# Dilated attention taken two units at a time, and retention outputs transposed in pairs

## The chip, the cores and the metric

The kernel runs on one core of a Trainium2 chip. The metric is device time of one execution in microseconds. Engines are named as in the profile: PE is the matrix engine (TensorE), with PEld for its weight loads; DVE is the vector engine, ACT the scalar engine, POOL GpSimd, and SP the engine whose queue issues most loads.

## What is computed

One layer of a decoder trunk for 512 tokens of 1024 features. The input projection feeds a retention mixer and a dilated attention; both outputs are gated, projected and added, and an MLP and a gated embedding follow. The change touches the dilated attention and the last step of the retention. Their part of the reference, cut:

```python
DIL_GROUPS = ((128, 1), (512, 4), (2048, 16))   # window, dilation; 8 heads of 64 each
def dilated_group(q, k, v, window, dilation):   # keys t - j*dilation, j = 0..window//dilation
    ...
    s = jnp.einsum('bcnqhe,bcnkhe->bcnhqk', qs, kk) * (hd ** -0.5)
    s = jnp.where(mask[None, :, None], s, -1e30)
    pr = jnp.exp(s - lse[..., None])
    o = jnp.einsum('bcnhqk,bcnkhe->bcnqhe', pr, vv)
...
yr = retention(rq, rk, rv, positions)
yr = rmsnorm(yr) * jax.nn.silu(rg)
ya_branch = yr.reshape(B, S, RET_V_W) @ w_ret_out[i]
```

## The kernel before

**Products in three passes.** Each 128x512 block of a large product is three matmuls (`PASSES`, L215): weights and features are split into a high and a low part of type fp32r, the high part by an ACT copy (L66) and the low part by a DVE subtraction (L69). Weights come in blocks of 512 KB through SP's queue (L82) into tiles of the pool `t` (26 tiles, which the attention's tiles share), and `prep_next` splits the next block while PE works.

**Fillers between the products.** `acc_tile` (L234) calls `pump()` after every three matmuls. `pump` hands out queued steps of other work at a given rate. The attention of a head group is such a list of steps: it is spread over 84 calls, and its matmuls stand between those of the next projections. A scheduler then sets the order on each engine from the order of the calls, its own estimate of when operands are there, and priorities; so a step's matmuls may stand some way from where they were handed out, and may be split up.

**One unit of attention.** `unit(t, p0)` covers 128 queries and, for the first head group, four heads (up to 256 keys, two blocks), for the other two groups all eight heads (128 keys). It has three steps. `scores` (matmuls at L475) multiplies q and k in fp32. A head has 64 features, so an instruction uses 64 of the array's 128 rows: even heads the upper half, odd heads the lower half, and each half writes a PSUM bank of its own. Then DVE adds the mask and takes the maximum of each head (L479), and ACT takes the exponentials (through L66). `flip` transposes the weights on PE (L495), and ACT copies them out of PSUM. `weigh` multiplies them with v (L506), and when all eight heads of 128 queries are done, DVE copies the sum (L511).

**Order of steps.** The list takes, for each unit in turn, `weigh` of the unit two before, `flip` of the one before, and `scores` of this one. There are eight units in the first head group and four in each of the other two.

**PSUM.** There are eight banks: four for the large products (`abank`, pool `pacc`), and four for everything else (`bank`, pool `pps`), handed out in turn. A bank is written again only when its reader is done.

**Retention.** At the end of each of four heads, the gated output of 128x512 values for each of four blocks of tokens is transposed by `flip(e)` (L814), four 128x128 transposes for each `e`; ACT copies the bank and sends it to DRAM. The four calls are handed out at 12, 14, 16 and 18 calls of `pump`.

Of the kernel before, what the change touches and what calls it, by code (L numbers as in the profile page):

```python
# [16 lines left out]
S, D, P = 512, 1024, 128  # L17
NT = S // P
# [13 lines left out]
def hybrid_block(ctx, tc, a, out):  # L32
    nc = tc.nc
# [12 lines left out]
    def nm(s):  # L46
        count[0] += 1
        return f"{s}{count[0]}"

    def big(shape=(P, D), dtype=F32):  # L50
        return pt.tile(list(shape), dtype, name=nm("t"), tag="t")

    def half(shape=(P, 512), dtype=F32):
        return psm.tile(list(shape), dtype, name=nm("s"), tag="s")

    def stat(n=1):
        return pst.tile([P, n], F32, name=nm("st"), tag=f"st{n}")

    def bank():
        return pps.tile([P, 512], F32, name=nm("b"), tag="ps")  # L60
# [4 lines left out]
    def act(o, i, f=AF.Copy, **kw):  # L65
        nc.scalar.activation(o, i, f, **kw)  # L66
# [39 lines left out]
    def new_w():  # L106
        return pw.tile([P, 2, 2, 512], F32R, name=nm("w"), tag="w")
# [90 lines left out]
    def later(lag, f):  # L198
        waiting.append([lag, f])
# [69 lines left out]
    ident = const.tile([P, P], F32, name="ident")  # L269
    xT = []  # L270
    for i in range(4):
        x = big((P, 2, 512))
# [55 lines left out]
    for i in range(4):  # L328
        w = new_w()
        r = pop()  # L330
        for j in range(2):
            f = 2 * i + j
# [11 lines left out]
    for t in range(NT):  # L344
        x = xr[t]
# [45 lines left out]
    def at(pair, i):  # L391
        return pair[i // 2][:, i % 2, :]
# [60 lines left out]
    def attention(g, qT, kT, v):  # L453
        n_g = pair_tiles()
        N.append(n_g)
        pairs = 2 if g == 0 else 4
        pvs = {}

        def unit(t, p0):
            nb = 2 if g == 0 and t > 0 else 1  # L460
            w = nb * P
            k0 = (t - nb + 1) * P
            s0, n = 2 * p0, 2 * pairs
            mk = masks[:, 2 - nb:2, :].rearrange("p a b -> p (a b)") if g == 0 else masks[:, g, :]
            mv, dv = M[g][:, t, s0:s0 + n], DEN[g][:, t, s0:s0 + n]
            got = {}

            def scores():
                sb = [bank(), bank()]
                sm = got["p"] = big((P, n, w))  # L470
                st = stat(8)
                for i in range(n):
                    q, hh = divmod(i, 2)
                    rows = slice(hh * 64, hh * 64 + 64)
                    nc.tensor.matmul(sb[hh][:, q * w:(q + 1) * w], at(qT, p0 + q)[rows, t * P:(t + 1) * P],  # L475
                                     at(kT, p0 + q)[rows, k0:k0 + w], start=True, stop=True)
                for i in range(n):
                    q, hh = divmod(i, 2)
                    nc.vector.tensor_tensor_reduce(  # L479
                        out=sm[:, i, :], in0=sb[hh][:, q * w:(q + 1) * w], in1=mk, scale=1.0, scalar=NEG,  # L480
                        op0=OP.add, op1=OP.max, accum_out=mv[:, i:i + 1])
                nc.vector.tensor_scalar(st[:, :n], mv, -0.125, None, op0=OP.mult)  # L482
                for i in range(n):
                    act(sm[:, i, :], sm[:, i, :], AF.Exp, bias=st[:, i:i + 1], scale=0.125,
                        accum_out=dv[:, i:i + 1])

            def flip():
                sm = got["p"]
                pT = got["t"] = big((P, n * w))
                for h0 in range(0, n * w, 512):  # L490
                    tb = bank()
                    m = min(512, n * w - h0)
                    for c in range(h0 // P, (h0 + m) // P):
                        i, j = divmod(c, nb)
                        nc.tensor.transpose(tb[:, c * P - h0:(c + 1) * P - h0], sm[:, i, j * P:(j + 1) * P], ident)  # L495
                    act(pT[:, h0:h0 + m], tb[:, :m])

            def weigh():
                if t not in pvs:
                    pvs[t] = [bank(), 0]  # L500
                pv = pvs[t][0]
                for i in range(n):
                    s = s0 + i
                    for j in range(nb):
                        c = i * nb + j
                        nc.tensor.matmul(pv[:, s * HD:(s + 1) * HD], got["t"][:, c * P:(c + 1) * P],  # L506
                                         at(v, t - nb + 1 + j)[:, s * HD:(s + 1) * HD],
                                         start=(j == 0), stop=(j == nb - 1))
                pvs[t][1] += n
                if pvs[t][1] == NS:  # L510
                    nc.vector.tensor_copy(at(n_g, t), pv)  # L511

            return scores, flip, weigh

        us = [unit(t, p0) for t in range(NT) for p0 in range(0, 4, pairs)]
        steps = []
        for i in range(len(us) + 2):
            for lag in (2, 1, 0):
                if 0 <= i - lag < len(us):
                    steps.append(us[i - lag][lag])  # L520
        return steps

    def stream_order(dst, src):
# [31 lines left out]
    yrd = [[pdr.tile([P, 512], F32, name=f"yrd{h}_{i}") for i in range(4)] for h in range(H)]  # L555
# [182 lines left out]
    def head(h):  # L738
        if h + 1 < H:
            load_decay(h + 1)  # L740
        qk = []
        held = []

        def qk_evac(t, ps):
            held.append(ps)
            if t % 2:
                qk.append(rope_pair(held[t - 1], held[t]))
        gemm(4, uT, qk_evac, wstat=True)
        qT, kT = qk
        if not h:  # L750
            flush()
            left_sums()
            for n in range(2):
                gemm(2, list_feed(yT), do_out(n, z1[n]), wstat=True)
        vh, sg, sc = {}, {}, []

        def v_evac(t, ps):
            o = vh[t] = big((P, 2, 512), F32R)
            r = rs0[:, t:t + 1]
            act(o[:, 0], ps, AF.Copy, scale=r)  # L760
            stt(o[:, 1], ps, r, o[:, 0].bitcast(F32), OP.mult, OP.subtract)

        def g_evac(t, ps):
            sg[t] = half()
            act(sg[t], ps, AF.Silu, scale=rs0[:, t:t + 1])

        def g_inner(t, x):
            sg[t] = x
            act(x, x, AF.Silu, scale=rs0[:, t:t + 1])

        def scores():
            for j in range(NT):
                w = S - j * P
                b = bank()
                n = 0
                for d in range(2):
                    for i1, i2 in PASSES:
                        nc.tensor.matmul(b[:, :w], kT[d][:, i1, j * P:(j + 1) * P], qT[d][:, i2, j * P:],
                                         start=(n == 0), stop=(n == 5))
                        n += 1  # L780
                s = half()
                tt(s[:, :w], b[:, :w], decay[h][:, :w], OP.mult)
                o = big((P, 2, 512), F32R)
                split(o[:, 0, :w], o[:, 1, :w], s[:, :w])
                sc.append(o)

        def retain(t):
            b = bank()
            n, last = 0, 3 * (t + 1) - 1
            for j in range(t + 1):  # L790
                c = (t - j) * P
                for i1, i2 in PASSES:
                    nc.tensor.matmul(b, sc[j][:, i1, c:c + P], vh[j][:, i2, :], start=(n == 0), stop=(n == last))
                    n += 1
            r = rstd([sumsq(b)], VD)
            return b, r

        def gate(t, br):
            stt(sg[t], br[0], br[1], sg[t])

        def last_part():
            for t in range(2):
                gate(t, retain(t))

        quartet(EARLY, quads,
                {"12": g_evac, 4: v_evac, 7: lambda t, x: v_evac(2 + t, x), "22": lambda t, x: g_inner(2 + t, x)},
                {"12": scores, "22": last_part})
        for t in (2, 3):
            gate(t, retain(t))

        def flip(e):
            b = bank()
            for t in range(NT):
                nc.tensor.transpose(b[:, t * P:(t + 1) * P], sg[t][:, e * P:(e + 1) * P], ident)  # L814
            o = half()
            act(o, b)
            nc.scalar.dma_start(yrd[h][e], o)

        for e in range(4):
            later(12 + 2 * e, lambda e=e: flip(e))  # L820

    z0d = [pdr.tile([P, 512], F32, name=f"z0d{i}") for i in range(KT)]
    ybd = [pdr.tile([P, 512], F32, name=f"ybd{i}") for i in range(KT)]
# [72 lines left out]
    for t in range(NT):  # L896
        x = big()
# [5 lines left out]
    for k in range(2):  # L903
        o = big((P, 2, 512), F32R)
# [157 lines left out]
    us = take(4)  # L1062
    hT = new_u()
    for t in range(NT):
        parts = []
        for n in range(2):
# [3 lines left out]
            f = part(t, n)  # L1070
# [8 lines left out]
    e = {n: pair_tiles() for n in range(2)}  # L1079
# [6 lines left out]
    parts = {}  # L1086
# [22 lines left out]
    us = take(4)  # L1109
    for t in range(NT):  # L1110
        parts_n = 1 if t < NT - 1 else 2
        w = 512 // parts_n
# [88 lines left out]
```

## Time and profile before

| what | value |
|---|---|
| time, median of three executions | 1212.58 us (1212.03 to 1213.17) |
| time of the profiled execution | 1212.39 us |
| its span, first to last instruction | 1210.6 us |
| PE busy | 1196.9 us, 5646 matmuls |
| PE weight loads busy | 989.3 us |
| DVE busy | 800.8 us |
| ACT busy | 579.1 us |
| granted clock of TensorE, mean | 0.997 |

The time of the profiled execution is 1.79 us more than its span; it lies 0.19 us under the median. PE runs nearly all of the span, so a change is read first from what stands in PE's order and how far apart its instructions start. Ends of matmuls are modelled by the profile, so their durations overlap; the starts are what can be subtracted from each other.

### The profile page before, as it was taken

How to read it: one execution, taken by the hardware profiler on the slowest of the kernel's cores; microseconds unless marked ns; L12 is line 12 of the kernel's file. 1: busy time of each engine (PE TensorE's matmuls, PEld its weight loads, DVE VectorE, ACT ScalarE, POOL GpSimd, SP SyncE). 2: the span in 40 equal slices, each digit the busy share in tenths (PEclk: the TensorE clock that was granted, in tenths of full speed). 3: DMA queues.
4: the chain of work that ended last, by engine and by line, in shares of the span. 5: the costliest groups of instructions: out<-in, count | busy, mean ns of one | idle time of the engine just before them, and what ended most of it. 6: DMA issues, size and time to landing. Idle time of an engine off the chain costs nothing. (4 is left out here: it accounts for less than half of the span.)

```text
span 1210.6 us, 15131 instructions
## 1 busy us (share of the span) xinstructions
PE 1196.9 (99%) x5646; PEld 989.3 (82%) x5646; DVE 800.8 (66%) x1199; ACT 579.1 (48%) x979; POOL 61.5 (5%) x112
## 2 busy tenths in 40 slices
PE   9999999999999999999999999999999999999996
PEld 7888788888888888888888888888888888888885
DVE  6743644654577895959768467673585775975696
ACT  7334444346744563535445532454553554553362
POOL 1002001000000000000000020020000000000210
PEclk9999999999999999999999999999999999999998
DMA  9432141332241543342335472727142251254401
GB/s 345 143 113 74 41 146 56 115 129 88 88 168 67 198 154 112 131 137 84 127 109 205 137 259 99 289 85 280 36 161 73 82 189 53 87 188 177 156 1 70
DMA packets 53322, 158.87 MB, mean 131 GB/s; under 512 B 8832, under 2 KB 9088, under 8 KB 53248
## 3 DMA queue, kind: packets, MB, share of 16 engines
q1 hardware_dynamic: 39552, 131.82, 30.9%
q10 hardware_dynamic: 9600, 14.53, 3.7%
q0 software_dynamic: 4096, 11.55, 2.6%
q8 instruction: 44, 0.72, 0.2%
q14 instruction: 30, 0.25, 0.1%
HBM read 139.47 MB, written 14.68 MB: 127 GB/s over the span
## 5 line engine op out<-in xcount | busy, mean ns | idle before, releaser
L69 DVE TENSOR_TENSOR w<-t,w 128x1024 fp32r<-128x1024 f32 (+1 forms) x248 | 295.7, 1204 | 144.7 <-ACT w L66 143.4
L66 ACT ACTIVATE w<-t 128x1024 fp32r<-128x1024 f32 (+1 forms) x248 | 256.9, 1044 | 261.9 <-PE a L234 93.7
L234 PE MATMUL a<-u,w 128*128 128x512 f32 x1536 | 369.0, 395 | 1.0 <-ACT t L66 1.0
L234 PEld LDWEIGHTS a<-u,w 128*128 128x128 f32 x1536 | 284.0, 188 | 62.1 <-issue 2.3
L69 DVE TENSOR_TENSOR t<-t,t 128x1024 f32<-128x1024 f32 (+4 forms) x179 | 185.0, 1058 | 26.3 <-ACT t L66 18.5
L706 PE MATMUL b<-w,t 128*128 128x512 f32 x696 | 162.5, 390 | 0.0
L706 PEld LDWEIGHTS b<-w,t 128*128 128x128 f32 x696 | 130.7, 188 | 27.0
L1030 PE MATMUL a<-u,w 128*128 128x512 f32 x576 | 134.0, 390 | 0.0
L1030 PEld LDWEIGHTS a<-u,w 128*128 128x128 f32 x576 | 108.2, 188 | 22.4
L234 PE MATMUL a<-w,u 128*128 128x512 f32 (+1 forms) x504 | 114.3, 384 | 0.2 <-DVE w L69 0.2
L234 PE MATMUL a<-t,w 128*128 128x512 f32 x480 | 110.5, 391 | 0.0
L234 PEld LDWEIGHTS a<-w,u 128*128 128x128 f32 x504 | 91.1, 189 | 18.4 <-DVE w L69 0.5
L69 DVE TENSOR_TENSOR t<-a,t 128x512 f32<-128x512 f32 x72 | 55.7, 776 | 75.3 <-ACT t L66 52.1
L234 PEld LDWEIGHTS a<-t,w 128*128 128x128 f32 x480 | 89.8, 188 | 18.8 <-DVE t L69 0.4
L234 PE MATMUL a<-w,t 128*128 128x512 f32 x432 | 99.6, 391 | 0.0
L234 PEld LDWEIGHTS a<-w,t 128*128 128x128 f32 x432 | 80.8, 188 | 16.7
L66 ACT ACTIVATE t<-t 128x512 fp32r<-128x512 f32 (+1 forms) x55 | 42.1, 787 | 37.7 <-DVE t L69 37.7
L66 ACT ACTIVATE t<-a 80x512 f32<-80x512 f32 (+1 forms) x32 | 18.9, 591 | 69.6 <-PE a L234 64.8
L66 ACT ACTIVATE t<-s 128x256 f32<-128x256 f32 (+3 forms) x94 | 41.8, 488 | 21.2 <-DVE s L69 20.3
L66 ACT ACTIVATE s<-a 128x512 f32<-128x512 f32 x56 | 32.7, 593 | 39.0 <-PE a L234 30.1
L69 DVE TENSOR_TENSOR s<-a,t 128x512 f32<-128x512 f32 x40 | 26.4, 687 | 37.1 <-PE a L234 30.2
L66 ACT ACTIVATE t<-t,st 128x128 f32<-128x128 f32 (+1 forms) x96 | 39.8, 416 | 22.5 <-DVE st L482 19.4
(119 smaller groups left out, 1004.3 us busy)
## 6 DMA issues: line engine op xcount, KB each, us to landing
t<-in_w_in_dram SPq DMA_DIRECT2D x104, 512.0 KB
t<-in_w_down_dram SPq DMA_DIRECT2D x38, 512.0 KB
t<-in_w_up_dram SPq DMA_DIRECT2D x32, 512.0 KB
t<-in_w_ret_out_dram SPq DMA_DIRECT2D x16, 512.0 KB
t<-in_x_dram SPq DMA_DIRECT2D x8, 512.0 KB
yrd<-s ACTq DMA_DIRECT2D x16, 256.0 KB
t<-yrd SPq DMA_DIRECT2D x16, 256.0 KB
t<-in_w_o_dram SPq DMA_DIRECT2D x8, 512.0 KB
```

The source lines that it names most:

```text
L66: nc.scalar.activation(o, i, f, **kw)
L69: nc.vector.tensor_tensor(o, x, y, op=op)
L234: nc.tensor.matmul(ps, l, r, start=(k == 0 and q == 0), stop=(k == n - 1 and q == 2))
L706: nc.tensor.matmul(ps[t], f(k, i, t), w[:, j, k2], start=(first and k == 0 and n == 0), stop=(k == 3 and n == 2), skip_group_check=not first)
L1030: nc.tensor.matmul(state["ps"][t], w[:, i, k2, t * P:(t + 1) * P], vT[:, x, k], start=(k == 0 and n == 0), stop=(k == 7 and n == 2))
```

## The change

`scores` is cut in two: `products` (the matmuls, now L473) and `weights` (the DVE and ACT work, L482 and L485). The list of steps no longer takes units one by one but in pairs. One entry of the list now runs `weigh` for both units of a pair, or `flip` for both, or `products` for both followed by `weights` for both. So there are twelve entries for the first head group instead of 24, and six for each of the others instead of twelve, spread over the same 84 calls. Transposes are now L498, products with v L509. In the retention, `flip(e0)` takes two banks, transposes eight blocks into them, and then copies and sends both; the two calls come at 12 and 16 calls of `pump`. Number, shapes and operands of the instructions stay as they were.

```diff
--- before.py
+++ after.py
@@ -465,15 +465,18 @@
             mv, dv = M[g][:, t, s0:s0 + n], DEN[g][:, t, s0:s0 + n]
             got = {}
 
-            def scores():
-                sb = [bank(), bank()]
-                sm = got["p"] = big((P, n, w))
-                st = stat(8)
+            def products():
+                sb = got["b"] = [bank(), bank()]
                 for i in range(n):
                     q, hh = divmod(i, 2)
                     rows = slice(hh * 64, hh * 64 + 64)
                     nc.tensor.matmul(sb[hh][:, q * w:(q + 1) * w], at(qT, p0 + q)[rows, t * P:(t + 1) * P],
                                      at(kT, p0 + q)[rows, k0:k0 + w], start=True, stop=True)
+
+            def weights():
+                sb = got["b"]
+                sm = got["p"] = big((P, n, w))
+                st = stat(8)
                 for i in range(n):
                     q, hh = divmod(i, 2)
                     nc.vector.tensor_tensor_reduce(
@@ -510,14 +513,23 @@
                 if pvs[t][1] == NS:
                     nc.vector.tensor_copy(at(n_g, t), pv)
 
-            return scores, flip, weigh
+            return products, weights, flip, weigh
 
         us = [unit(t, p0) for t in range(NT) for p0 in range(0, 4, pairs)]
+
+        def both(i, parts):
+            def f():
+                for k in parts:
+                    for x in us[2 * i:2 * i + 2]:
+                        x[k]()
+            return f
+
         steps = []
-        for i in range(len(us) + 2):
-            for lag in (2, 1, 0):
-                if 0 <= i - lag < len(us):
-                    steps.append(us[i - lag][lag])
+        m = len(us) // 2
+        for i in range(m + 2):
+            for lag, parts in ((2, (3,)), (1, (2,)), (0, (0, 1))):
+                if 0 <= i - lag < m:
+                    steps.append(both(i - lag, parts))
         return steps
 
     def stream_order(dst, src):
@@ -808,16 +820,18 @@
         for t in (2, 3):
             gate(t, retain(t))
 
-        def flip(e):
-            b = bank()
-            for t in range(NT):
-                nc.tensor.transpose(b[:, t * P:(t + 1) * P], sg[t][:, e * P:(e + 1) * P], ident)
-            o = half()
-            act(o, b)
-            nc.scalar.dma_start(yrd[h][e], o)
-
-        for e in range(4):
-            later(12 + 2 * e, lambda e=e: flip(e))
+        def flip(e0):
+            b = {e: bank() for e in (e0, e0 + 1)}
+            for e in b:
+                for t in range(NT):
+                    nc.tensor.transpose(b[e][:, t * P:(t + 1) * P], sg[t][:, e * P:(e + 1) * P], ident)
+            for e in b:
+                o = half()
+                act(o, b[e])
+                nc.scalar.dma_start(yrd[h][e], o)
+
+        for e0 in (0, 2):
+            later(12 + 2 * e0, lambda e0=e0: flip(e0))
 
     z0d = [pdr.tile([P, 512], F32, name=f"z0d{i}") for i in range(KT)]
     ybd = [pdr.tile([P, 512], F32, name=f"ybd{i}") for i in range(KT)]
```

The order on PE, first head group (b is a PSUM bank of the attention, a one of a large product, u the features, w a weight block, t_254 and t_255 are keys and t_252 and t_253 queries). Before, the score products of one unit:

```order
L234 MATMUL a_1177<-u_134,w_1138 128x512 x6
L234 MATMUL a_1229<-u_134,w_883 128x512 x6
L475 MATMUL b_1236<-t_254,t_252 128x256 x2
L234 MATMUL a_1229<-u_134,w_1103 128x512 x5
L475 MATMUL b_1237<-t_254,t_252 128x256 x2
L234 MATMUL a_1229<-u_134,w_1103 128x512
L234 MATMUL a_1229<-u_134,w_1114 128x512 x3
```

Now, those of two units:

```order
L234 MATMUL a_1031<-u_134,w_856 128x512 x3
L473 MATMUL b_1047<-t_254,t_252 128x256
L473 MATMUL b_1048<-t_254,t_252 128x256
L473 MATMUL b_1047<-t_254,t_252 128x256
L473 MATMUL b_1048<-t_254,t_252 128x256
L473 MATMUL b_1053<-t_255,t_253 128x256
L473 MATMUL b_1054<-t_255,t_253 128x256
L473 MATMUL b_1053<-t_255,t_253 128x256
L473 MATMUL b_1054<-t_255,t_253 128x256
L234 MATMUL a_1031<-u_134,w_856 128x512 x3
```

Before, the unit's four products stood as two of one bank and, after five large matmuls, two of the other; now eight stand together and the two banks of a unit (the two halves of the array's rows) alternate.

The order on PE in the second head group, around the first transposes (b<-ident). Before, of the first unit:

```order
L234 MATMUL a_1577<-w_1166,u_134 128x512 x3
L495 MATMUL b_1582<-ident,t_1531 128x128 x4
L234 MATMUL a_1577<-w_1166,u_134 128x512
L495 MATMUL b_1588<-ident,t_1531 128x128
L234 MATMUL a_1577<-w_1166,u_134 128x512
L495 MATMUL b_1588<-ident,t_1531 128x128
L234 MATMUL a_1577<-w_1166,u_134 128x512
L495 MATMUL b_1588<-ident,t_1531 128x128
L234 MATMUL a_1577<-w_1362,u_134 128x512
L495 MATMUL b_1588<-ident,t_1531 128x128
L234 MATMUL a_1577<-w_1362,u_134 128x512 x5
```

Now, of the first pair, with the last score product ahead of it:

```order
L473 MATMUL b_1563<-t_709,t_707 128x128
L234 MATMUL a_1548<-w_1153,u_134 128x512 x3
L234 MATMUL a_1548<-w_1366,u_134 128x512 x6
L234 MATMUL a_1548<-w_1377,u_134 128x512 x6
L234 MATMUL a_1548<-w_1388,u_134 128x512 x6
L234 MATMUL a_1670<-u_134,w_1417 128x512 x6
L498 MATMUL b_1693<-ident,t_1572 128x128 x4
L498 MATMUL b_1699<-ident,t_1572 128x128 x4
L498 MATMUL b_1706<-ident,t_1591 128x128 x4
L498 MATMUL b_1712<-ident,t_1591 128x128 x4
L234 MATMUL a_1724<-u_134,w_1417 128x512 x2
```

Before, the eight transposes stood four together and four singly between the products; now sixteen, of two units, stand in one row, 27 large matmuls behind the score products.

The order on ACT at the same place (t,d<-t,st are exponentials, t<-a,rs copies of a projection to v, w<-t the high parts of weight blocks). Before:

```order
L66 ACTIVATE t_1531,d_247<-t_1531,st_1532 128x128 x4
L66 ACTIVATE t_1463<-a_1522,rs_182 128x512
L66 ACTIVATE t_1531,d_247<-t_1531,st_1532 128x128 x4
L66 ACTIVATE t_1581<-b_1582 128x512
L66 ACTIVATE t_1581<-b_1588 128x512
L66 ACTIVATE w_1597<-t_1389 128x1024
L66 ACTIVATE w_1608<-t_1400 128x1024
```

Now:

```order
L66 ACTIVATE t_1572,d_247<-t_1572,st_1573 128x128 x8
L66 ACTIVATE t_1591,d_247<-t_1591,st_1592 128x128 x4
L66 ACTIVATE t_1463<-a_1548,rs_182 128x512
L66 ACTIVATE t_1591,d_247<-t_1591,st_1592 128x128 x4
L66 ACTIVATE w_1613<-t_1380 128x1024
L66 ACTIVATE w_1624<-t_1391 128x1024
L66 ACTIVATE w_1635<-t_1420 128x1024
```

Before, eight exponentials stood ahead of the transposes' two copies, and the weight copies behind; now sixteen exponentials stand in a row, cut only by a copy of v, and the next weight copies come behind all of them.

## Rows read from the trace of the kernel before

**Rows 1.** The page of the whole program: busy time of each engine (share of the span, number of instructions), and the clock granted to TensorE in 40 slices of the span, in tenths of full speed.

```profile
PE 1196.9 (99%) x5646; PEld 989.3 (82%) x5646; DVE 800.8 (66%) x1199; ACT 579.1 (48%) x979; POOL 61.5 (5%) x112
PEclk9999999999999999999999999999999999999998
```

**Rows 2.** The waits of PE over the whole program, first and last of six rows (engine, line, what it waited for: us in total, times, longest us).

```profile
PE b L268 <- DVE s L265: 1.5, 1, 1.5
PE b L475 <- DVE t L69: 0.2, 1, 0.2
```

**Rows 3.** The windows view of PE for two stretches: the one from the first score product to the last product with v, and one of 100 us that holds nothing but 128x512 products (stretch, its length in us, busy us and number of instructions, granted clock as a share of full speed, DMA share, GB/s).

```profile
83.20:336.28 253.08, 252.86 (x1372) 1.00 0.27 88
690.00:790.00 100.00, 100.00 (x443) 1.00 0.57 207
```

**Rows 4.** PE's groups of instructions by line and shape in the stretch 83.2 to 336.28 us (xcount | busy us, mean ns of one | idle us before them). One L234 row lies across the edge of the stretch.

```profile
L234 PE MATMUL a<-u,w 128*128 128x512 f32 x669 | 166.3, 400 | 0.0
L234 PE MATMUL a<-w,u 128*128 128x512 f32 x151 | 37.3, 398 | 0.0
L506 PE MATMUL b<-t,t 128*128 128x64 f32 x240 | 28.7, 272 | 0.0
L495 PE MATMUL b<-ident,t 128*128 128x128 f32 x120 | 21.0, 277 | 0.0
L475 PE MATMUL b<-t,t 64*128 64x128 f32 x144 | 12.0, 291 | 0.2 <-DVE t L69 0.2
L475 PE MATMUL b<-t,t 64*128 64x256 f32 x48 | 10.4, 407 | 0.0
```

**Rows 5.** The timeline of PE for one unit of the second head group (start us, us until the end that the profile models, what runs, how many in a row). Rows of L475, L506 and the fp32 products at the start show two records for each instruction of the program.

```profile
215.59 1.16 PE L475 MATMUL b<-t,t 64*128 64x128 f32 x16
216.69 5.06 PE L234 MATMUL a<-u,w 128*128 128x512 f32 x21
221.59 1.89 PE L506 MATMUL b<-t,t 128*128 128x64 f32 x16
223.29 5.06 PE L234 MATMUL a<-u,w 128*128 128x512 f32 x21
228.18 1.03 PE L495 MATMUL b<-ident,t 128*128 128x128 f32 x8
228.97 5.02 PE L234 MATMUL a<-u,w 128*128 128x512 f32 x21
```

**Rows 6.** The same timeline where two groups of eight score records follow each other closely.

```profile
184.94 0.71 PE L475 MATMUL b<-t,t 64*128 64x128 f32 x8
185.58 0.73 PE L234 MATMUL a<-w,u 128*128 128x512 f32 x2
186.25 0.71 PE L475 MATMUL b<-t,t 64*128 64x128 f32 x8
```

**Rows 7.** The same timeline for score products with 256 keys: first four instructions that alternate between the two halves of the array's rows, then two instructions of one half alone.

```profile
109.85 1.13 PE L475 MATMUL b<-t,t 64*128 64x256 f32 x8
110.92 3.02 PE L234 MATMUL a<-u,w 128*128 128x512 f32 x12
145.82 1.13 PE L475 MATMUL b<-t,t 64*128 64x256 f32 x4
146.88 1.43 PE L234 MATMUL a<-u,w 128*128 128x512 f32 x5
```

**Rows 8.** The same timeline where single transposes stand between single 128x512 products.

```profile
274.17 0.27 PE L495 MATMUL b<-ident,t 128*128 128x128 f32 x1
274.19 0.48 PE L234 MATMUL a<-u,w 128*128 128x512 f32 x1
274.51 0.27 PE L495 MATMUL b<-ident,t 128*128 128x128 f32 x1
```

**Rows 9.** The timeline of PE at the first head's retention outputs.

```profile
462.98 0.60 PE L814 MATMUL b<-ident,s 128*128 128x128 f32 x4
463.34 1.64 PE L234 MATMUL a<-u,w 128*128 128x512 f32 x6
464.81 0.60 PE L814 MATMUL b<-ident,s 128*128 128x128 f32 x4
```

**Rows 10.** The timeline of DVE and ACT for one unit of eight heads: two of its reductions, the scaling of the maxima, the first two exponentials, and the copies of eight transposes out of PSUM (the last row merges two).

```profile
200.39 0.29 DVE L479 CUSTOM_DVE_ANT_0 t<-b,masks 128x128 f32<-128x128 f32 x1
200.61 0.28 DVE L479 CUSTOM_DVE_ANT_0 t<-b,masks 128x128 f32<-128x128 f32 x1
201.78 0.17 DVE L482 TENSOR_SCALAR st<-m 128x8 f32<-128x8 f32 x1
201.98 0.40 ACT L66 ACTIVATE t<-t,st 128x128 f32<-128x128 f32 x1 [2.97 <-DVE st L482]
202.38 0.39 ACT L66 ACTIVATE t<-t,st 128x128 f32<-128x128 f32 x1
210.49 1.09 ACT L66 ACTIVATE t<-b 128x512 f32<-128x512 f32 x2 [3.96 <-PE b L495]
```

**Rows 11.** The groups of ACT and of DVE for the two halves of a weight split in the stretch 83.2 to 336.28 us (columns as in Rows 4).

```profile
L66 ACT ACTIVATE w<-t 128x1024 fp32r<-128x1024 f32 x35 | 35.8, 1053 | 7.9 <-PE a L234 7.8
L69 DVE TENSOR_TENSOR w<-t,w 128x1024 fp32r<-128x1024 f32 x35 | 41.3, 1217 | 14.2 <-ACT w L66 14.1
```

**Rows 12.** The waits of SP's queue of loads in the same stretch, the row for buffers that products with v release (columns as in Rows 2).

```profile
SPq L82 <- PE b L506: 53.4, 4, 24.0
```

## The prediction

> **What bounds the kernel now.** I read the page first. PE is busy 99% of the span, its granted clock stands at nine tenths or more in all slices but the last, so at the upper of its two levels, and DVE and ACT are busy two thirds and half [rows 1]. The waits say the same: what PE waited for over the whole program sums to a few us, from 1.5 us down to 0.2 us [rows 2]. So there is hardly any waiting to remove. A change pays if PE's own instructions stand closer together, and costs if PE begins to wait. I therefore took starts, not durations, since the records of PE overlap.
>
> A stretch with nothing but 128x512 products holds 443 records in 100 us [rows 3]. About two of them lie across its edges, so one takes 0.227 us. The attention's stretch is 253.08 us long [rows 3] and holds 819 such products beside 552 small records [rows 4]. The large ones need 819 x 0.227 = 185.9 us. The other **67.2 us** are what the small records cost there, and all of it lies on the path that sets the end.
>
> **What each kind costs.** A turn is the time from the start of one small group to the start of the next, less 0.227 us for each large product between them.
> - Products with v: 221.59 to 228.18 us is 6.59 us, less 21 products (4.77), leaves 1.82 us for 16 records, 0.114 each [rows 5]. 240 of them [rows 4] are 27.3 us.
> - Transposes: a single one costs 0.34 - 0.227 = 0.113 us [rows 8]. Four together cost 1.83 - 6 x 0.227 = 0.47 us, of which 0.36 pass before the next product starts and 0.11 after it [rows 9]. Eight take 0.79 us before it [rows 5], so 0.90 in all, 0.112 each. Whether they stand singly or together matters little. 120 of them [rows 4] are 13.6 us.
> - Scores: what is left, 67.2 - 27.3 - 13.6 = **26.3 us** for 192 records.
>
> Why are the scores dear? Eight records take 0.64 us until the next large product [rows 6], sixteen take 1.10 us [rows 5]: one more record is only 0.0575 us. But the turn of eight is 1.31 - 2 x 0.227 = 0.86 us [rows 6], so 0.40 us is paid for each visit, however few records it has. The second loss is that two instructions on different halves of the rows run side by side: with 256 keys, eight records that alternate take 1.07 us, and four of one half alone take 1.06 us [rows 7]. The 256-key records that alternate cost (1.07 - 0.64) / 8 = 0.054 us more than the others, 0.111 us.
>
> **Scores in pairs.** In the order on PE, the score products stand in 24 groups before and in 9 now, and in each of the nine the halves alternate. With the same prices: 9 x 0.40 + 144 x 0.0575 + 48 x 0.111 = 3.6 + 8.3 + 5.3 = 17.2 us, so 26.3 - 17.2 = **9.1 us gained**. The trace has no group of 32 score records; that it goes on at 0.0575 is taken from the step from 8 to 16.
>
> The fixed 0.40 us stands in the rows whatever its cause. The Trainium skill ("TensorEngine Tiling (Array Packing)", Key Properties) says that changing the tiling mode drains TensorE, while tiles of one mode load and multiply in parallel; by that rule, the trace agrees: only the 64-row products pay for a visit, and the transposes do not. "TensorE: Matmul & The Clock Gate" (Single matmul latency) gives a constant of 166 ns at the full clock, so two drains in a visit would be 0.33 us, an estimate from that page; 15 fewer visits would then give 5.0 us where the row's price gives 6.0, and the sum below would end 1 us later.
>
> **The other parts.** Products with v stand in 9 groups instead of 17, most of them of 32 records. 0.114 a record may hold a small fixed part: between 0 and 0.5 us in all, I take 0.2. The transposes of the attention, sixteen in a row: 0 to 0.3 us, I take 0.1. The retention's 64 transposes now stand in eights: 64 x (0.117 - 0.112) = 0.3 us at most [rows 5, 9], I take 0.2. The retention's outputs are issued to DRAM from ACT's queue about where they were, and their readers come much later. Gain so far: 9.1 + 0.2 + 0.1 + 0.2 = **9.6 us**.
>
> **What the change adds: a wait.** The reductions and exponentials of two units now stand in a row, and everything behind them on DVE and ACT comes later, the split of the next weights above all. The tightest place is the first pair of the second head group: 27 large products stand between its scores and its transposes. Count from the start of the scores. The first unit's scores take 0.4 + 16 x 0.0575 = 1.3 us, its eight reductions 0.22 us each (1.8), the scaling 0.2 [rows 10], so the first exponential starts at 3.3 us. Sixteen at 0.40 us [rows 10] and the copy of v between them (0.55, as the copies of the transposes [rows 10]) end at 10.3 us. PE takes 2.2 us for the scores, 6.1 for the products, and is at the last transpose at 8.3 + 15 x 0.112 = 10.0 us: it waits 0.3 us. Behind the exponentials ACT makes the high part of the next weight block, 1.05 us [rows 11], done at 11.3 us. PE has only two products ready after the transposes, so it waits there from about 10.9 us: 0.4 us more. With signals between the engines I take **1.0 us** here. If DVE first has to finish a split (1.22 us [rows 11]) it is 2.2 us; if DVE and ACT start a little earlier it is nothing. The first pair of the third head group has the same 27 products, and the first of the first group has 20 products but half as many exponentials of each unit; I take nothing for them, up to 2.2 and 1 us for the range. Elsewhere 42 or more products, or other small work beside 18 or more, cover it.
>
> **The sum.** 1212.4 us for the profiled execution (0.2 us under the median of the three runs, so the same) less 9.6 plus 1.0 gives **1203.8 us**.
>
> **Rivals.**
> 1. *The wait grows.* Every pair's transposes find ACT not done, and weight splits come late behind two units' work: 1 to 2.3 us at three places, or 0.4 to 0.9 us at each of the eight, takes back 3 to 7 us: 1206 to 1210 us. For it speaks that the bursts double. Against it: DVE and ACT are idle for a third and a half of the time [rows 1].
> 2. *Weights arrive late, and the gain goes.* SP's loads wait for attention tiles: 53.4 us in four waits for what products with v release [rows 12]. Two units in flight hold these tiles longer, by a turn of products with v (1.8 us) and 21 to 42 large products (4.8 to 9.5 us). A load that lands 7.5 to 12 us later than needed would eat the sum or more: 1210 to 1215 us. Against it: the loads waited 24 us at the longest [rows 12], and yet PE hardly waited.
> 3. *Slower: four banks.* A pair's scores now write all four banks of the small pool, and so do its transposes. Each must wait until the last reader of all four is done, where before two units' banks could overlap. After a group of scores, 16 reductions need 16 x 0.22 = 3.5 us; four copies need 2.2 us [rows 10]. Behind are 18 to 27 products (4.1 to 6.1 us) at the tight places. If DVE or ACT has three or four splits queued ahead (1.05 to 1.22 us each [rows 11]), the next group starts 2 to 3 us late; at six of the pairs that is 12 to 18 us, so 1214 to 1221 us. It decides against the change from 1.2 us on at each of the eight pairs. Against it: splits stand behind the reductions in most places of the order, and most gaps are longer.
>
> A rule of the Trainium skill speaks for this third rival: "Perfetto Trace Analysis" (Optimizing Tensor Performance, Matmuls) wants independent groups to rotate through different banks, so that emptying one overlaps with the next. In this trace, with two banks for each group, PE's waits are too small to show what it costs to break the rule.
>
> That the change doesn't do what it says is nearly excluded: the order shows the groups as described, but for four that one or two large products split.
>
> **How the numbers follow.** The forecast, 1201.2 to 1205.5 us, gets 0.70. Rival 1 gets 0.19, rival 2 0.06, rival 3 0.05. The range reaches from 1201.2 us (no wait, and the upper ends of the small gains: 10.2 us, and 1 us for the rounding of 0.227 over 819 products) to 1208 us, which takes in the larger part of rival 1. A measurement of this kernel can tell about 0.2%, 2.4 us, from no change: faster means under 1210.2 us. That is the forecast and rival 1, 0.89; rival 2 is mostly within 0.2%, 0.07; slower, 0.04.
>
> **What would show it.** In the profile after, the small records of the attention's stretch should cost 57 to 59 us by the same subtraction; sixteen score instructions should take about 2.0 us until the next large product; and PE should wait for ACT around the first transposes of the second head group, about 1 us. Waits of PE for DVE at scores or for loads would show rivals 3 and 2. The prediction is wrong if 32 score records cost more than two groups of 16, or if the waits exceed 3 us.

## The result and the profile after

| what | before | after |
|---|---|---|
| median of four executions on one chip | 1212.43 us (1212.03 to 1213.17) | 1202.40 us (1202.26 to 1202.87) |
| profiled execution, its span | 1212.39, 1210.6 us | 1202.87, 1201.1 us |
| attention's stretch, large products in it | 253.08 us, 819 | 241.46 us, 807 |
| what its 552 small records cost | 67.2 us | 58.3 us |

The ratio of the times is 0.9915, with a 95% interval of 0.9900 to 0.9931: the kernel became 10.0 us faster, where 8.6 us were predicted. The two profiled executions lie 9.5 us apart, and the traces are read against that.

The page of after, the lines that answer to [rows 1]: PE has the same instructions and is as full as before, at the same clock.

```profile
PE 1187.5 (99%) x5646; PEld 988.0 (82%) x5646; DVE 800.9 (67%) x1199; ACT 576.7 (48%) x979; POOL 61.5 (5%) x112
PEclk9999999999999999999999999999999999999998
```

The windows view of PE in after, from the first score product to the end of the last product with v, and then its groups by line and shape in that stretch (columns as in [rows 3] and [rows 4]). One L234 row lies across the edge.

```profile
85.59:327.05 241.46, 241.25 (x1360) 1.00 0.28 92
```

```profile
L234 PE MATMUL a<-u,w 128*128 128x512 f32 x669 | 158.6, 394 | 0.2 <-ACT w L66 0.2
L234 PE MATMUL a<-w,u 128*128 128x512 f32 x139 | 33.2, 394 | 0.0
L509 PE MATMUL b<-t,t 128*128 128x64 f32 x240 | 27.7, 273 | 0.0
L498 PE MATMUL b<-ident,t 128*128 128x128 f32 x120 | 15.3, 274 | 0.1
L473 PE MATMUL b<-t,t 64*128 64x128 f32 x144 | 9.6, 280 | 0.0
L473 PE MATMUL b<-t,t 64*128 64x256 f32 x48 | 6.0, 389 | 0.0
```

The subtraction of the prediction, done again: 241.46 - 807 x 0.227 = **58.3 us** for the same small records. So 8.9 of the 9.5 us were gained inside this stretch. Of the rest, 0.3 us lie ahead of it, and 0.3 us behind it. That the stretch is shorter by 11.6 us instead of 8.9 is no gain of its own: 12 of the large products now stand ahead of it.

The timeline of PE at the first pair of the second head group, and at two later groups, one of sixteen transposes and one of sixteen score instructions (columns as in [rows 5]).

```profile
183.05 2.06 PE L473 MATMUL b<-t,t 64*128 64x128 f32 x32
185.03 5.06 PE L234 MATMUL a<-w,u 128*128 128x512 f32 x21
189.93 1.53 PE L234 MATMUL a<-u,w 128*128 128x512 f32 x6
191.30 2.28 PE L498 MATMUL b<-ident,t 128*128 128x128 f32 x16
193.34 0.71 PE L234 MATMUL a<-u,w 128*128 128x512 f32 x2
194.20 12.76 PE L234 MATMUL a<-u,w 128*128 128x512 f32 x55 [0.15 <-ACT w L66]
206.89 2.06 PE L473 MATMUL b<-t,t 64*128 64x128 f32 x32
208.88 9.14 PE L234 MATMUL a<-u,w 128*128 128x512 f32 x39
...
231.69 1.91 PE L498 MATMUL b<-ident,t 128*128 128x128 f32 x16
233.36 9.78 PE L234 MATMUL a<-u,w 128*128 128x512 f32 x42
```

Sixteen score instructions (32 records) take 208.88 - 206.89 = 1.99 us until the next large product, where sixteen records took 1.10 us [rows 5]. With the 0.20 us that the large products on both sides are held up, a group of 32 costs 2.19 us in the starts of the trace.

The added wait is here too. Sixteen transposes take 233.36 - 231.69 = 1.67 us where nothing holds them, and 193.34 - 191.30 = 2.04 us at the first pair: 0.37 us of waiting. Then two products take 194.20 - 193.34 = 0.86 us, of which 0.45 are theirs and 0.11 are left over from the transposes [rows 9]: 0.30 us more. ACT in the same place shows the cause (start us, us, what runs): the first and the last of sixteen exponentials, then the high part of the next weight block.

```profile
186.35 0.40 ACT L66 ACTIVATE t<-t,st 128x128 f32<-128x128 f32 x1 [3.18 <-DVE st L485]
...
192.72 0.39 ACT L66 ACTIVATE t<-t,st 128x128 f32<-128x128 f32 x1
193.10 1.04 ACT L66 ACTIVATE w<-t 128x1024 fp32r<-128x1024 f32 x1
```

The first exponential starts 3.30 us after the scores, as the prediction counted; the last ends 10.1 us after them (10.3 in the prediction), and the weight block is done at 11.1 us (11.3). PE goes on with the products 0.06 us later. The waits of PE over the whole program, first and last two of six rows, do not even list the wait at the transposes, which is spread over three of their steps; the last row is the end of the wait at 194.20 us. No row is for a score product or for a load.

```profile
PE b L268 <- DVE s L265: 1.5, 1, 1.5
...
PE a L234 <- DVE w L69: 0.2, 1, 0.2
PE a L234 <- ACT w L66: 0.2, 1, 0.2
```

### The profile page after: what moved, and what is told of

The parts are those of the page before. It is cut to its first block, busy times and chain, and to the rows that moved or that the text cites. A ratio compares the mean times of both kernels' runs of the same rounds, so it can differ in the third digit from the quotient of the medians.

```text
span 1201.1 us, 15103 instructions
## 1 busy us (share of the span) xinstructions
PE 1187.5 (99%) x5646; PEld 988.0 (82%) x5646; DVE 800.9 (67%) x1199; ACT 576.7 (48%) x979; POOL 61.5 (5%) x112
## 5 line engine op out<-in xcount | busy, mean ns | idle before, releaser
L234 PE MATMUL a<-u,w 128*128 128x512 f32 x1536 | 359.4, 392 | 1.0 <-ACT t L66 0.9
L234 PEld LDWEIGHTS a<-u,w 128*128 128x128 f32 x1536 | 285.6, 188 | 62.2 <-ACT t L66 1.1
L718 PEld LDWEIGHTS b<-w,t 128*128 128x128 f32 x696 | 130.6, 188 | 27.1
L1044 PE MATMUL a<-u,w 128*128 128x512 f32 x576 | 134.0, 389 | 0.0
L234 PE MATMUL a<-w,u 128*128 128x512 f32 (+1 forms) x504 | 112.8, 382 | 0.2 <-DVE w L69 0.2
L234 PE MATMUL a<-t,w 128*128 128x512 f32 x480 | 109.9, 390 | 0.0
L234 PEld LDWEIGHTS a<-w,u 128*128 128x128 f32 x504 | 91.3, 189 | 18.7 <-DVE w L69 0.5
L234 PEld LDWEIGHTS a<-t,w 128*128 128x128 f32 x480 | 89.9, 188 | 18.9 <-DVE t L69 0.4
L234 PE MATMUL a<-w,t 128*128 128x512 f32 x432 | 99.6, 390 | 0.0
L234 PEld LDWEIGHTS a<-w,t 128*128 128x128 f32 x432 | 80.7, 188 | 16.7
L305 POOL TENSOR_TENSOR st<-st,mhalf 128x1 f32<-128x1 f32 x28 | 16.2, 578 | 569.1 <-DVE st L303 567.9
```

What stands on the lines that cost most here:

```text
L234: nc.tensor.matmul(ps, l, r, start=(k == 0 and q == 0), stop=(k == n - 1 and q == 2))
L305: nc.gpsimd.tensor_tensor(r, v, mhalf[:, :1], op=OP.pow)
L718: nc.tensor.matmul(ps[t], f(k, i, t), w[:, j, k2], start=(first and k == 0 and n == 0), stop=(k == 3 and n == 2), skip_group_check=not first)
L1044: nc.tensor.matmul(state["ps"][t], w[:, i, k2, t * P:(t + 1) * P], vT[:, x, k], start=(k == 0 and n == 0), stop=(k == 7 and n == 2))
```

## The experiments

Each time stands beside that of the kernel before on the same chip: 1213.05 us (1211.23 to 1213.93) for the first four runs, 1213.03 us (1211.80 to 1213.88) for the others. "Small records" is always the subtraction above, made on that run's own stretch. An expectation's theory A is that of the prediction: a visit of PE to the 64-row products costs 0.40 us, and halves that alternate run side by side.

### Only the scores in pairs

In this kernel and the next, the retention transposes singly, as before. Of both edits only the list of steps is shown; `scores` is cut in two as in the change.

```diff
+        for i in range(len(us) + 2):
+            if 0 <= i - 2:
+                steps.append(run((us[i - 2], 3)))
+            if 0 <= i - 1 < len(us):
+                steps.append(run((us[i - 1], 2)))
+            if i < len(us):
+                pair = us[i:i + 2] if i % 2 == 0 else []
+                steps.append(run(*((x, k) for k in (0, 1) for x in pair)))
```

> Starts from the changed kernel; only the score products (and their reductions and exponentials) are taken in pairs, transposes and products with v go unit by unit as before, and the retention outputs singly. In the order the scores stand in 13 groups (9 in the changed kernel, 24 before). Theory A, that the gain lies in the number of score groups (0.40 us each) and in both halves of the array's rows running side by side: 4 more groups and some halves alone, 1205.0 to 1206.5 us. Theory B, that pairing the transposes and the products with v gives a good part of the gain: 1207.5 us or more.

Measured: 1209.62 us (1208.01 to 1212.96), ratio 0.9978 [0.9968, 0.9988]. Small records 63.2 us. By its number the run speaks for B, but the order on PE was not the one intended. The timeline of PE in the first head group and at the first pair of the second:

```profile
99.37 1.99 PE L473 MATMUL b<-t,t 64*128 64x256 f32 x12
101.29 1.67 PE L234 MATMUL a<-u,w 128*128 128x512 f32 x6
103.11 1.13 PE L473 MATMUL b<-t,t 64*128 64x256 f32 x4
104.17 0.96 PE L234 MATMUL a<-u,w 128*128 128x512 f32 x3
...
183.24 1.16 PE L473 MATMUL b<-t,t 64*128 64x128 f32 x14
184.86 1.39 PE L473 MATMUL b<-t,t 64*128 64x128 f32 x18 [0.47 <-DVE t L69]
186.18 5.06 PE L234 MATMUL a<-w,u 128*128 128x512 f32 x21
```

The scheduler split the pairs of the first head group into groups of 12, 8 and 4 records, several of one half alone: four records take 1.06 us until the next product. The 256-key scores cost 10.8 us in seven groups, where the changed kernel pays 6.4 us in three. The pair at 183 us cost 3.14 instead of 2.19 us, since its keys, which DVE writes, were late (the same wait stood in [rows 2] with 0.2 us). These 4.4 and 0.9 us, less the wait of 0.7 us at the transposes, which this order does not have, are 4.6 of the 4.9 us to after; the rest is not accounted for. The run can't tell A from B; the next can.

### All but the scores in pairs

```diff
+        for i in range(0, len(us) + 4, 2):
+            if 0 <= i - 4:
+                steps.append(run(*((x, 3) for x in us[i - 4:i - 2])))
+            if 0 <= i - 2 < len(us):
+                steps.append(run(*((x, 2) for x in us[i - 2:i])))
+            for x in us[i:i + 2]:
+                steps.append(run((x, 0), (x, 1)))
```

> Starts from the changed kernel; transposes and products with v in pairs, score products unit by unit (each unit a step of its own), retention outputs singly. In the order the scores stand in 16 groups, none of one half alone and none cut by transposes. Theory A: 7 groups more than the changed kernel, 2.8 us, less the wait at the second head group, that is 1204.0 to 1205.5 us, so most of the gain without one score being paired. Theory B, that the scores' pairing itself is the gain: 1209 us or more.

Measured: 1205.99 us (1205.05 to 1206.74), ratio 0.9945 [0.9930, 0.9960]; small records 60.3 us. The timeline of PE in the second head group:

```profile
180.68 1.16 PE L473 MATMUL b<-t,t 64*128 64x128 f32 x16
181.77 7.78 PE L234 MATMUL a<-w,u 128*128 128x512 f32 x33
189.48 1.16 PE L473 MATMUL b<-t,t 64*128 64x128 f32 x16
```

The median lies 0.5 us above A's range, on a chip where the kernel before takes 0.6 us more; B, with 1209 us or more, falls. No two units' scores stand together, and yet 6.9 of the 8.9 us are there. The prices say why: in this order the scores make 16 visits instead of 24 and none is of one half alone, which is worth 26.3 - (16 x 0.40 + 8.3 + 5.3) = 6.3 us by the prediction's own terms.

### The second unit's scores three products later

```diff
+        if "next" in fill:
+            fill.pop("next")()
...
+            def f():
+                x[0]()
+                fill["next"] = second
```

> The changed kernel with one edit: the score products of the second unit of a pair are handed out one call of pump (three large products) after those of the first; all else stays in pairs. In the order there are 16 score groups. Theory A, 0.40 us for each visit: 7 more are 2.8 us, 1205.2 us, and about 2.8 us more for the small records in the attention's stretch. Theory D, that the fixed cost is one of short groups among other fp32 work and not of each visit: 1202.4 us.

Measured: 1207.63 us (1206.51 to 1208.58), ratio 0.9959 [0.9944, 0.9974]; small records 61.1 us, 2.8 more than after, with 16 visits instead of 9. The timeline of PE (L475 and L236 are the scores and the products here):

```profile
186.16 1.16 PE L475 MATMUL b<-t,t 64*128 64x128 f32 x16
187.25 0.97 PE L236 MATMUL a<-w,u 128*128 128x512 f32 x3
188.15 1.16 PE L475 MATMUL b<-t,t 64*128 64x128 f32 x16
189.24 4.38 PE L236 MATMUL a<-w,u 128*128 128x512 f32 x18
```

2.8 us for seven more visits are 0.40 us each, the price in the prediction (0.1 of the 2.8 us is a longer wait at the second head group's transposes). The pair shown says the same: 189.24 - 186.16 less three products is 2.40 us in two visits, against 1.99 in one. Theory A's price stands, and D falls. By 1213.05 - 10.0 + 2.8 the time would be 1205.8 us, and it is 1.8 us more. These are not in the attention. In the profiled execution, the longest of the four (1208.58 us), the first score stands at 87.61 us, where it stood at 85.59 us in after with the same work ahead of it, and 0.9 us more pass behind the last product with v. The last group of experiments shows that the start varies.

### The halves not alternating, in runs of two and four, and in runs of four and eight

First, within each unit, all even heads and then all odd ones; then the same over a pair (even heads of both units, then odd heads of both). Only the first edit is shown; in the second, `products` takes the half as an argument.

```diff
-                for i in range(n):
-                    q, hh = divmod(i, 2)
+                for j in range(n):
+                    hh, q = divmod(j, n // 2)
```

> The changed kernel with one edit: a unit's score products run through all even heads first and then through all odd heads, so that instructions of one half of the array's rows follow each other; the groups are the same 9. Theory A, with halves side by side as a part of the gain: each pair of instructions loses the overlap but at the seam, 8 to 12 us, 1211 to 1214.5 us. Theory C, that only the number of groups counts: no change, 1202.4 us.

> The changed kernel with one edit: of a pair of units all even heads' score products run first, then all odd heads', so instructions of one half follow each other in runs of eight (four in the first head group), where runs of four cost 0.77 us a group of 32 records and runs of two 0.1 us. Theory F, that the array overlaps halves only as far as PE runs ahead by a few instructions: runs of eight lose 1.1 to 1.6 us in each of four groups and runs of four 0.5 to 1 us in each of three, 6 to 9.5 us, 1208.5 to 1212 us. Theory C, that the order of halves in a group hardly matters: under 4 us, below 1206.5 us.

Measured: 1206.15 us (1205.80 to 1206.90), ratio 0.9949 [0.9932, 0.9965], for the first; 1212.33 us (1211.06 to 1214.20), ratio 0.9996 [0.9987, 1.0006], for the second. Small records 61.3 and 67.0 us. The timelines of PE of the first and of the second (scores L473 and L474):

```profile
183.38 2.82 PE L473 MATMUL b<-t,t 64*128 64x128 f32 x32
186.13 5.10 PE L234 MATMUL a<-w,u 128*128 128x512 f32 x21
```

```profile
99.09 2.96 PE L474 MATMUL b<-t,t 64*128 64x256 f32 x16
101.99 5.10 PE L234 MATMUL a<-u,w 128*128 128x512 f32 x21
...
187.18 3.50 PE L474 MATMUL b<-t,t 64*128 64x128 f32 x32
190.60 5.07 PE L234 MATMUL a<-w,u 128*128 128x512 f32 x21
```

The visits are as many as in after and hold as many records (but for the first pair's two in the second run, 4 and 12 instead of 8 and 8); only the order in them differs. Until the next product, 32 records take 1.99 us when the halves alternate, 2.75 in runs of four instructions, 3.42 in runs of eight. A group of 256-key scores costs 2.13, 2.23 (runs of two) and 3.10 us (runs of four). The first run missed my 8 to 12 us by far: I had priced it as if no two products of different halves could meet, but they overlap nearly as well when two of one half stand in a row, and still in part when four do. The second is as F had it: 4 x 1.44 + 3 x 0.97 = 8.7 us in the small records, nearly the whole gain undone by order alone; C falls. Its median lies 0.3 us above F's range, where the kernel before takes 0.6 us more on this chip.

### The changed kernel again, and its wait removed

The lists of steps are started earlier against the calls of `pump`, so that more products stand between a pair's scores and its transposes: in the second and third head groups alone, then also later in the first.

```diff
-        filler(attention(g, qT, kT, vc), 84, 10)
+        filler(attention(g, qT, kT, vc), 84, 5 if g else 10)
```

```diff
-        filler(attention(g, qT, kT, vc), 84, 10)
+        filler(attention(g, qT, kT, vc), 84, 5 if g else 12)
```

> The changed kernel once more, beside the ones below: 1202.4 us, up to 1203.2 us if this chip is as slow as the one of the last experiments. Its small records in the attention's stretch cost 58.3 us as before; the two waits in the first 30 us, which differ from run to run, may move the time by 1 to 2 us, and no theory says more on them.

> The changed kernel, with the steps of the second and third head group handed out five calls of pump earlier. In the order 42 large products stand between each scores group and its transposes, where the first pair of both groups had 27, and no row of transposes is split. Theory A, that the wait at the second head group's first transposes (0.7 us in the trace) comes from 27 products being too few for sixteen exponentials and the split behind them: it goes, small records 57.6 us, 0.7 us faster than the changed kernel of this chip. Theory E, that the wait comes from DVE and ACT being late by other work: it stays at 0.5 to 1 us somewhere, and the time too.

> As the last one, and the first head group's steps start two calls of pump later, so that its first two units' scores stand together (8 groups of scores instead of 9). Theory A: another visit of 0.40 us and 0.1 us of entry less, small records 57.1 us, 1.2 us faster than the changed kernel of this chip. Theory D (no price for a visit): as the last one.

| kernel | median, us | ratio | small records, us |
|---|---|---|---|
| changed kernel again | 1203.25 (1201.93 to 1203.82) | 0.9917 [0.9903, 0.9932] | 58.3 |
| 5 for two groups | 1203.50 (1202.72 to 1203.54) | 0.9919 [0.9905, 0.9934] | 57.5 |
| 5, and 12 for the first | 1202.37 (1201.66 to 1202.98) | 0.9911 [0.9897, 0.9926] | 56.8 |

The timeline of PE of the last one, the first pair of the first and of the second head group:

```profile
87.37 1.16 PE L473 MATMUL b<-t,t 64*128 64x128 f32 x16
88.46 5.07 PE L234 MATMUL a<-w,u 128*128 128x512 f32 x21
...
179.50 2.06 PE L473 MATMUL b<-t,t 64*128 64x128 f32 x32
181.49 8.46 PE L234 MATMUL a<-w,u 128*128 128x512 f32 x36
...
191.15 1.91 PE L498 MATMUL b<-ident,t 128*128 128x128 f32 x16
192.81 7.51 PE L234 MATMUL a<-u,w 128*128 128x512 f32 x32
```

With 42 products behind the first pair of the second group (36 of them in the row shown) instead of 27, the transposes take 192.81 - 191.15 = 1.66 us and the wait is gone, in this run and in the one before it: the small records fall by 0.8 us, as A had it, and E falls. With the 12, the first pair is one group instead of two, and they fall by 0.7 us more, where 0.5 were expected. The whole times can't confirm these 0.8 and 1.5 us (with the 5 alone the median is even 0.25 us above the changed kernel's), and the waits of PE in the first 83 us, ahead of the attention, say why. Of after, of the changed kernel again, and of the run with the scores apart, the rows for ACT:

```profile
PE a L234 <- ACT t L66: 0.9, 1, 0.9
```

```profile
PE a L234 <- ACT w L66: 1.5, 1, 1.5
PE a L234 <- ACT t L66: 1.0, 1, 1.0
```

```profile
PE a L236 <- ACT t L66: 1.8, 1, 1.8
...
PE a L236 <- ACT w L66: 0.8, 1, 0.8
```

The work ahead of the attention is the same in all three. These waits for ACT sum to 0.9, 2.5 and 2.6 us, and the first score stands at 85.59, 87.02 and 87.61 us. What follows the attention varies too: the second of the three ends only 0.9 us later than the first, since it takes 0.5 us less behind the last product with v. The last kernel has the lowest median and the fewest us in small records, but 0.9 us less than the changed kernel on the same chip lies within that spread.

## Why the prediction was right, step by step

The groups of after, summed by kind from the starts in the trace, against the prediction's terms:

| term | predicted, us | measured, us |
|---|---|---|
| scores, 9 visits | 17.2 | 17.1 |
| products with v | 27.1 | 26.9 |
| transposes without a wait | 13.5 | 13.5 |
| wait at the second head group | 1.0 | 0.7 |
| their sum, and the stretch's 58.3 by subtraction | 58.8 | 58.2 |
| retention, gain | 0.2 | 0.15 |

**Scores.** The term that carries the forecast held: 9 visits, 32 records that go on at (2.19 - 0.40) / 32 = 0.056 us each, and 9.1 us gained. The test that the prediction named against itself, that 32 records cost more than two groups of sixteen, came out the other way: 2.19 us against 2 x 1.29 in the run with the scores apart. The waits of PE's weight loads in after show a stop at the visits: ahead of eight of the nine they stand still for 0.34 us each, and for nothing that the profile shows.

```profile
PEld b L473 <- issue: 2.7, 8, 0.4
```

The rule on drains of the Trainium skill ("TensorEngine Tiling (Array Packing)", Key Properties) agrees with the trace as far as that only 64-row products pay for a visit. The 0.33 us, the estimate that was worked out for it with the constant of the Trainium skill ("TensorE: Matmul & The Clock Gate", Single matmul latency), is too little: the seven visits cost 0.40 us each.

**What the name of the change hides.** Of the 9.1 us only 7 x 0.40 = 2.8 come from two units' scores standing together. The 6.3 us are from scores that are no longer split up between the products: eight visits fewer (3.2 us), and the rest, 3.1 us, mostly from groups of one half alone that are gone. This is why pairing everything but the scores gave most of the gain, and the run that paired nothing but the scores, where the first head group's were split again, little. The prediction counted visits in the order, so its sum was right; it did not say that most of the gain was not due to two units' scores standing together.

Why the scheduler splits the scores in one list of steps and not in the other was not tried. For the 256-key groups of one half alone a count of banks fits the orders. In the first head group, a sum of products with v keeps one of the four small banks from the first unit of 128 queries to the second; a unit's transposes want two, and its scores two more (a pair's, four). Before, the four groups of four records of one half stand where such a sum is open: those of [rows 7] at 145.82 us and the next at 148.24, between products with v at 138.25 and 150.32 us. In the run that paired only the scores, all three 256-key pairs begin so. There the last four records of the first of them wait for DVE's reductions (L482), which release a bank: 0.58 us at the weight load, where it is 0.35 us for the twelve records ahead of them.

```profile
103.11 0.73 PEld L473 LDWEIGHTS b<-t,t 64*128 64x128 f32 x4 [0.58 <-DVE m L482]
```

Where the products with v of both units stand in one step, the sum is closed at once, and no run of that kind has a group of one half alone that the list did not ask for. By this count it is the pairing of products with v that keeps the scores whole; that is read off the orders and not shown by a run.

**Small terms.** Products with v have hardly any fixed part: 32 records cost 3.58 us, eight cost 0.90, 0.112 each in either. Nine instead of seventeen visits can have saved only about 0.1 us of the 0.2 that I took; that the term came out below 27.1 us all the same is the price of a record, 0.112 instead of 0.114 us. Eight transposes of the retention cost 0.883 us, four 0.451: 0.02 us for each of eight pairs, 0.15 us. This was read from the trace and not run by itself.

**The wait** came where it was put, for the reason given, and 0.3 us smaller, most of it because ACT was done 0.2 us earlier. No wait followed at the first pair of the third head group or of the first.

**The rivals.** Rival 1 would have shown as PE waiting at three or more of the pairs; it waits at one. Of rivals 2 and 3 there is no sign in after: PE waits for no load in the stretch, and for no bank at the scores. A pair on all four banks thus cost nothing here. The rule on rotating banks of the Trainium skill ("Perfetto Trace Analysis", Optimizing Tensor Performance, Matmuls) is not refuted by that, only without a price where 18 or more products stand behind a pair's group. With six products behind twelve records, in the run that paired only the scores, it shows in the row above.

**The size.** The profiled execution ended 0.9 us below the sum of 1203.8 us: 0.5 us are the small records of the table, 0.3 us lie ahead of the stretch, where waits vary anyway, and 0.1 us behind it. The median is 0.5 us below the profiled execution. That the kernels before and after waited about alike at the start in their profiled executions (1.0 and 0.9 us for ACT) is luck: in the other profiled execution of the changed kernel, the first score stands 1.4 us later.

## What to carry to other kernels

Price small matmuls between large ones by starts: a stretch less its large products at their steady step, then a fixed price for a visit and a price for each further record, and count visits in the order that the scheduler really makes. Products that use half of the rows belong into few groups whose halves alternate; a pair of steps helps less by standing together than by no longer being split. And where a burst doubles, count the engine behind it to the microsecond: three terms from three rows put the wait in the right place.

## What was not expected of the hardware

- Products on the two halves of the rows overlap though they don't strictly alternate. For 32 records, runs of two instructions were not tried; runs of four cost 0.76 us and runs of eight 1.44 us more than alternating ones. For sixteen 256-key records, runs of two cost 0.10 us and runs of four 0.97 us more.
- Waits for ACT near the start of the kernel sum to 0.9 us in one execution and to 2.5 us in another of the same code; the difference is more than the last two experiments changed.
